# Storing m tiles 61 and 62 of a matmul-minus-matrix kernel in two transfers, of 120 and of 8 partitions

## The chip, the core and the metric

The kernel runs on one core of a Trainium2 chip. A core has a matrix engine (TensorE, PE in the profile) with its weight loads (PEld), a vector engine (VectorE, DVE), a scalar engine (ScalarE, ACT), GpSimd (POOL) and SyncE (SP), which here issues every DMA. The transfers are carried out by 16 DMA engines that the whole core shares. The metric is the device time of one execution in microseconds; the median over several runs is compared. The profile of one execution comes with its own time.

## The reference

```python
x:         (16, 512, 1024) float32     # 8192 rows of 1024 in all
weight:    (1024, 768)     float32
sub_value: (16, 512, 768)  float32
out = (np.matmul(x, weight) - sub_value).astype(np.float32)
```

## The kernel before

The 8192 rows are cut into 64 m tiles of 128 rows. Rows are not dealt to tiles in sequence: in each stretch of eight tiles (1024 rows) partition p holds eight consecutive rows, one for each tile. So one partition's rows of several neighbouring tiles lie next to each other in HBM, and a transfer of n tiles moves one run of n x 3,072 bytes for each partition (n x 4,096 bytes for x). This is what `view` (line 128) builds.

One m tile passes through these steps. Its x rows land in `x_ring` (16 slots). ScalarE casts them to fp16 (`cast`, L317). They are transposed, on TensorE for most tiles (`transposes`, L335, and a ScalarE copy out of PSUM, L348) and on VectorE for 18 of them (`transposes_dve`, L368). Then come 16 matmuls of 384 columns into `po_b` (`matmuls`, L198 and the weight loads of L397). The rows of sub_value have meanwhile landed in `so_ring` (32 slots); `finish` (L417) subtracts them on VectorE from the product, in place, and the slot then holds the output. From there it is stored.

All transfers are issued by SP in the order of the hand-written list `TRANSFERS` (line 29): loads of x, weight ("w") and sub_value ("s") and stores ("o") of mostly eight tiles each. The last entries are

```python
    ('o', 24, 8), ('o', 32, 8), ('s', 56, 8), ('o', 40, 8), ('o', 48, 8), ('o', 56, 5),
    ('o', 61, 2), ('o', 63, 1),
```

so the last three stores take tiles 56 to 60, tiles 61 and 62, and tile 63. `issue` (line 241) writes SP's instruction for each entry: a wait, for a store on the `finish` of its last tile, and one DMA instruction (L298; L262 for the weights). Each transfer signals a semaphore, called a lane, that `lane` (line 229) hands out; every lane counts to 16 for one transfer.

At the end (lines 520 to 527) SP first waits for every lane that nothing has waited for yet, but for the lane of the last store. Then the section is closed, with a barrier over all engines, and only after it SP waits for the last store, that of tile 63:

```python
    for one in left:
        if one is not last:
            nc.sync.wait_ge(one["sem"], one["value"])
    section.close()
    with tc.tile_critical(sync_engine=mybir.EngineType.SP, no_gpsimd_drain=True):
        nc.sync.wait_ge(last["sem"], last["value"])
```

Of the kernel before, what the change touches and what calls it, by code (L numbers as in the profile page):

```python
# [8 lines left out]
P = 128  # L9
# [5 lines left out]
NX, NSO = 16, 32  # L15
# [21 lines left out]
]  # L37


class Queue:  # L40
# [65 lines left out]
def kernel(  # L106
# [7 lines left out]
    nc = tc.nc  # L114
# [3 lines left out]
    out_flat = out.flatten_outer_dims()  # L118

    M_TOT, K = x_flat.shape  # L120
    _, N = weight.shape
    n_mt = M_TOT // P
# [5 lines left out]
    def view(flat, at, n):  # L128

        first, size = next(one for one in SEGMENTS if one[0] <= at < sum(one))  # L130
        assert at + n <= first + size
        rows = flat[first * P : (first + size) * P].rearrange("(p j) c -> p j c", p=P, j=size)
        return rows[:, at - first : at - first + n]
# [6 lines left out]
    def sbuf(name, shape, dtype):  # L140
        return ctx.enter_context(nc.sbuf_tensor(name, shape, dtype)).ap()
# [11 lines left out]
    so_ring = sbuf("so_ring", [P, NSO, N], F32)  # L153
# [11 lines left out]
    counter = {}  # L165
# [4 lines left out]
    def count(name):  # L170
        so_far[name] += 1
        return (counter[name], 1)

    sp, pe = Queue(nc, nc.sync), Queue(nc, nc.tensor)
    act, dve, pool = Queue(nc, nc.scalar), Queue(nc, nc.vector), Queue(nc, nc.gpsimd)
# [6 lines left out]
        out=along, data0=ones, data1=ones, initial=0.0, op0=mybir.AluOpType.mult, op1=mybir.AluOpType.add,  # L182
    ), waits=[(counter["ident"], 1)], then=count("ident"))
    dve.add(lambda: nc.vector.transpose(across, along), waits=[(counter["ident"], 3)], then=count("ident"))  # L184
    for a in range(P // Q):
        here = slice(a * Q, (a + 1) * Q)
        dve.add(lambda here=here: nc.vector.tensor_tensor(  # L187
            out=ident[here, here], in0=along[here], in1=across[here], op=mybir.AluOpType.is_equal,
# [16 lines left out]
    landed = {}  # L205
    cast_at, evac_at, pair_at, turn_at, mul_at, finish_at, w_at = {}, {}, {}, {}, {}, {}, {}
# [16 lines left out]
    done = {"w": set(), "x": set(), "s": set(), "o": set(), "cast": set(), "finish": set()}  # L223
    staged = {}
    lanes = []
    of_x, of_s, of_o = {}, {}, {}
    known = set()

    def lane(tag):

        for one in lanes:
            if one["tags"] <= known:
                break
        else:
            one = {"sem": tc.alloc_semaphore(f"lane{len(lanes)}"), "value": 0, "tags": set()}
            lanes.append(one)
        one["value"] += 16
        one["tags"].add(tag)
        return one["sem"], one["value"]

    def issue():
        nonlocal known
        while todo:
            kind, at, n = todo[0]
            span = set(range(at, at + n))
            old = {t - NX if kind == "x" else t - NSO for t in span}
            need, by = {
                "w": (set(), "o"),
                "x": ({t for t in old if t >= 0}, "cast"),
                "s": ({t for t in old if t >= 0}, "o"),  # L250
                "o": (span, "finish"),
            }[kind]
            if not need <= done[by]:
                return
            todo.pop(0)
            done[kind] |= span
            if kind == "w":

                first = NSO - 2 * (n_c - at)
                st = so_ring[:, first : first + 2]  # L260
                sem, value = lane((kind, at))
                sp.add(lambda st=st, at=at: nc.sync.dma_start(out=st, in_=w_c[at]), then=(sem, 16))  # L262
                for r in range(2):
                    dve.add(
                        lambda at=at, r=r, st=st: nc.vector.tensor_copy(out=w_sb[:, at, r], in_=st[:, r]),  # L265
                        waits=[(sem, value)], then=count("w"),
                    )
                    staged[first + r] = so_far["w"]
                w_at[at] = so_far["w"]
                continue  # L270
            ring, size, flat = {
                "x": (x_ring, NX, x_flat), "s": (so_ring, NSO, sub_flat), "o": (so_ring, NSO, out_flat)
            }[kind]
            here = ring[:, at % size : at % size + n]
            there = view(flat, at, n)
            waits = []
            if kind == "x" and need:
                waits.append((counter["cast"], max(cast_at[t] for t in need)))
                last = max(need, key=lambda t: cast_at[t])
                known |= {tag for t, tag in of_x.items() if t in cast_at and cast_at[t] <= cast_at[last]}  # L280
            if kind == "s":
                for t in need:
                    waits.append(landed["o", t])
                    known.add(of_o[t])
                for t in span:
                    if t % NSO in staged:
                        waits.append((counter["w"], staged.pop(t % NSO)))
                        known |= {("w", c) for c in w_at if w_at[c] <= waits[-1][1]}
            if kind == "o":
                waits.append((counter["finish"], max(finish_at[t] for t in need)))  # L290
                known |= {of_s[t] for t in finish_at if finish_at[t] <= max(finish_at[u] for u in need)}
            sem, value = lane((kind, at))
            for t in span:
                landed[kind, t] = (sem, value)
                {"x": of_x, "s": of_s, "o": of_o}[kind][t] = (kind, at)
            if kind == "o":
                here, there = there, here
            sp.add(lambda here=here, there=there: nc.sync.dma_start(out=here, in_=there), waits, (sem, 16))  # L298

    def cast(mi):  # L300
        assert mi in done["x"]
        done["cast"].add(mi)
        x_in = x_ring[:, mi % NX]
        first = mi - mi % 2
        waits = [landed["x", mi]]
        if first in ON_DVE:
            if mi == first:
                b, before = take("x16p", N16P, mi)
                if before is not None:
                    waits.append((counter["pair"], pair_at[before]))  # L310
            to = x16p_b[:, slot["x16p", first], mi - first]
        else:
            b, before = take("x16", N16, mi)
            if before is not None:
                waits.append((counter["turn"], turn_at[before]))
            to = x16_b[:, b]
        act.add(lambda: nc.scalar.copy(out=to, in_=x_in), waits, count("cast"))  # L317
        cast_at[mi] = so_far["cast"]
        issue()
# [92 lines left out]
    def finish(mi):  # L412
        assert mi in done["s"]
        done["finish"].add(mi)
        o = so_ring[:, mi % NSO].rearrange("p (h n) -> p h n", h=2)
        po = po_b[:, slot["po", mi]]
        dve.add(lambda: nc.vector.tensor_tensor(  # L417
            out=o, in0=po[:, :, :NS], in1=o, op=mybir.AluOpType.subtract
        ), [landed["s", mi], (counter["mul"], mul_at[mi])], count("finish"))
        finish_at[mi] = so_far["finish"]  # L420
        issue()

    issue()


# [59 lines left out]
    for mi in range(HEAD + (EARLY is not None), n_mt):  # L485
# [3 lines left out]
        t = mi + TA  # L489
# [32 lines left out]
    for one in left:  # L522
        if one is not last:
            nc.sync.wait_ge(one["sem"], one["value"])
    section.close()
    with tc.tile_critical(sync_engine=mybir.EngineType.SP, no_gpsimd_drain=True):
        nc.sync.wait_ge(last["sem"], last["value"])
# [30 lines left out]
```

## Time and profile before

| | |
|---|---|
| median of 4 runs | 210.36 us (210.15 to 210.57) |
| profiled execution, its time | 210.45 us |
| profiled execution, its span | 208.6 us |
| PE busy | 195.4 us (94%) |
| DVE busy | 128.2 us (61%) |
| ACT busy | 109.0 us (52%) |
| the DMA queue's packets, share of 16 engines | 97.8% |
| bytes moved | 87.08 MB, 417 GB/s over the span |
| store of tiles 56 to 60: 1,920 KB, issue to landing | 10.1 us |
| store of tiles 61 and 62: 768 KB, issue to landing | 6.2 us |
| store of tile 63: 384 KB, issue to landing | 4.5 us |

The span runs from the first to the last instruction; the time of a run has some two microseconds more around it. A busy share is an average over the whole span, and engines overlap. "Issue to landing" runs from the start of SP's DMA instruction to the last of the sixteen completions of that transfer. The DMA share counts the time that packets took, over 16 engines; 1.00 is all sixteen busy, and one engine alone is 0.06.

### The profile page before, as it was taken

To read this page: it belongs to the slowest core of one execution; us is meant where nothing else is said; L and a number is where in the kernel's file an instruction comes from. 1 tells how busy PE (TensorE), PEld (TensorE's weight loads), DVE (VectorE), ACT (ScalarE), POOL (GpSimd) and SP (SyncE) were. 2 spreads that over 40 slices of the span, in tenths; PEclk is the share of its full clock that TensorE was granted. 3 is DMA by queue.
4 is the path that set the end of the run, shared out by engine and by line. 5 is a ranking of instruction groups with operands and counts; after the bars stand their busy time and mean duration, and the time that the engine had idled before them with its cause. 6 is when DMAs were issued, how large, how long until landed. Compare 5 with 4: busy or idle time off the path is not lost.

```text
span 208.6 us, 2612 instructions
## 1 busy us (share of the span) xinstructions
PE 195.4 (94%) x1234; PEld 75.5 (36%) x700; DVE 128.2 (61%) x224; ACT 109.0 (52%) x113; POOL 1.0 (0%) x7
## 2 busy tenths in 40 slices
PE   6999699969999999999999999999999999999960
PEld 0234243324434433443443443343344344334310
DVE  2323224975994795598399379469839938952330
ACT  3555659506673761944645576193564737507300
POOL 1000000000000000000000000000000000000000
PEclk9999999999999999999999999999999999999997
DMA  6999999999999999999999999999999999999993
GB/s 210 417 426 431 435 426 429 459 423 421 434 446 459 375 429 448 446 408 432 467 408 424 448 415 424 471 426 418 430 454 399 435 443 434 410 443 448 410 413 124
DMA packets 5476, 87.08 MB, mean 417 GB/s; under 512 B 608, under 2 KB 608, under 8 KB 1888
## 3 DMA queue, kind: packets, MB, share of 16 engines
q1 hardware_dynamic: 5472, 87.03, 97.8%
q8 instruction: 1, 0.02, 0.0%
q14 instruction: 3, 0.02, 0.0%
HBM read 61.87 MB, written 25.17 MB: 417 GB/s over the span
## 4 chain that ended last, share of the span: by engine, by line
PE 75%; DMA 13%; DVE 6%; SPq 3%; issue 1%; DVEq 0%
PE po_b L198 67%; DMA so_ring<-in_sub_value_dram 13%; PE pt_b L335 8%; DVE xtp_b L368 3%; DVE so_ring L417 2%; SPq L298 2%; SPq L262 1%; SPq L553 0%; DVEq L59 0%; SPq L138 0%
## 5 line engine op out<-in xcount | busy, mean ns | idle before, releaser
L198 PE MATMUL po_b<-w_sb,xt_b 128*128 128x384 f16 x704 | 126.0, 326 | 0.9 <-DVE w_sb L265 0.8
L417 DVE TENSOR_TENSOR so_ring<-po_b,so_ring 128x768 f32<-128x768 f32 x64 | 60.8, 957 | 59.5 <-PE po_b L198 40.0
L348 ACT COPY xt_b<-pt_b 128x1024 f16<-128x1024 f16 x44 | 44.5, 1012 | 65.7 <-PE pt_b L335 64.8
L368 DVE STREAM_TRANSPOSE xtp_b<-x16p_b 32x256 f32<-32x256 f32 x144 | 62.7, 435 | 2.3
L198 PE MATMUL po_b<-w_sb,xtp_b 128*128 128x384 f16 x320 | 61.3, 326 | 1.9 <-DVE xtp_b L368 1.7
L397 PEld LDWEIGHTS <-xt_b 128*128 128x128 f16 x352 | 34.4, 98 | 58.6 <-issue 55.3
L317 ACT CAST x_b<-x_ring 128x1024 f16<-128x1024 f32 x46 | 47.2, 1048 | 4.8 <-DMA x_ring<-in_x_dram 4.8
L335 PE MATMUL pt_b<-ident,x_b 128*128 128x128 f32 x184 | 47.5, 274 | 1.9 <-ACT x_b L317 1.8
L335 PEld LDWEIGHTS pt_b<-ident,x_b 128*128 128x128 f32 x184 | 25.4, 141 | 45.0 <-issue 36.6
L317 ACT CAST x16p_b<-x_ring 128x1024 f16<-128x1024 f32 x18 | 18.8, 1046 | 14.8 <-DMA x_ring<-in_x_dram 14.8
L397 PEld LDWEIGHTS <-xtp_b 128*128 128x128 f16 x160 | 15.7, 98 | 20.4 <-issue 18.3
L265 DVE CAST w_sb<-so_ring 128x768 f16<-128x768 f32 x8 | 4.1, 557 | 11.6 <-DMA so_ring<-in_weight_dram 11.6
L198 PE MATMUL po_b<-idle_x,idle_w 128*128 128x512 f16 x26 | 7.9, 454 | 1.7 <-POOL idle_x L178 1.7
L348 ACT COPY xtp_b<-pt_b 128x1024 f16<-128x1024 f16 x2 | 2.0, 1012 | 2.5 <-PE pt_b L335 2.5
L317 ACT ACT_TABLE_LOAD x1 | 1.3, 1283 | 0.9 <-SPq L138 0.9
L427 PEld LDWEIGHTS <-idle_w 128*128 128x128 f16 x4 | 0.4, 100 | 1.7 <-POOL idle_x L178 1.7
L187 DVE TENSOR_TENSOR ident<-along,across 32x32 f32<-32x32 f32 x4 | 0.7, 183 | 0.1
L179 DVE MEMSET ones<- 128x32 f32 x1 | 0.1, 85 | 1.0 <-SPq L138 1.0
L178 POOL MEMSET idle_x<- 128x512 f16 x1 | 0.5, 530 | 0.0
L499 ACT CAST stub<-ident 128x1 f16<-128x1 f32 x2 | 0.4, 194 | 0.0
L184 DVE STREAM_TRANSPOSE across<-along 128x32 f32<-128x32 f32 x1 | 0.2, 211 | 0.0
L476 POOL MEMSET mark<- 128x1 f32 x1 | 0.1, 99 | 24.0 <-ACT xtp_b L348 24.0
(7 smaller groups left out, 1.0 us busy)
## 6 DMA issues: line engine op xcount, KB each, us to landing
so_ring<-in_sub_value_dram SPq DMA_DIRECT2D x7, 3072.0 KB, 24.2
out_dram<-so_ring SPq DMA_DIRECT2D x7, 3072.0 KB, 26.6
x_ring<-in_x_dram SPq DMA_DIRECT2D x5, 4096.0 KB, 23.1
x_ring<-in_x_dram SPq DMA_DIRECT2D x2, 2048.0 KB, 27.6
so_ring<-in_weight_dram SPq DMA_DIRECT2D x4, 768.0 KB, 8.4
x_ring<-in_x_dram SPq DMA_DIRECT2D x1, 3072.0 KB, 28.6
x_ring<-in_x_dram SPq DMA_DIRECT2D x2, 1024.0 KB, 25.0
out_dram<-so_ring SPq DMA_DIRECT2D x1, 1920.0 KB, 10.1
```

The costliest lines, as they stand in the source:

```text
L178: pool.add(lambda: nc.gpsimd.memset(idle_x, 0.0), then=count("idle"))
L187: dve.add(lambda here=here: nc.vector.tensor_tensor(out=ident[here, here], in0=along[here], in1=across[here], op=mybir.AluOpType.is_equal, ...
L198: return nc.tensor.add_instruction(mybir.InstMatmult(name=nc.get_next_instruction_name(), engine=full.engine, ins=list(full.ins), outs=lis ...
L262: sp.add(lambda st=st, at=at: nc.sync.dma_start(out=st, in_=w_c[at]), then=(sem, 16))
L265: lambda at=at, r=r, st=st: nc.vector.tensor_copy(out=w_sb[:, at, r], in_=st[:, r]),
L298: sp.add(lambda here=here, there=there: nc.sync.dma_start(out=here, in_=there), waits, (sem, 16))
L317: act.add(lambda: nc.scalar.copy(out=to, in_=x_in), waits, count("cast"))
L335: pe.add(lambda: nc.tensor.transpose(words, from_, ident), waits, count("turn") if last else None)
L348: act.add(lambda: nc.scalar.copy(out=to, in_=pt_b[:, b]), waits, count("evac"))
L368: dve.add(lambda: nc.vector.transpose(xt[b * Q : (b + 1) * Q, :, a * Q : (a + 1) * Q], x16[a * Q : (a + 1) * Q, :, b * Q : (b + 1) * Q],), ...
L397: pe.add(lambda weights=weights: nc.tensor.ldweights(weights, tile_position=(0, 0)), [w for w in waits if w[0] in ready])
L417: dve.add(lambda: nc.vector.tensor_tensor(out=o, in0=po[:, :, :NS], in1=o, op=mybir.AluOpType.subtract), [landed["s", mi], (counter["mul"] ...
```

## The change

The store of tiles 61 and 62 becomes two transfers on the same queue, of partitions 0 to 119 and of partitions 120 to 127. Both move two tiles (6,144 bytes for a partition). Every other transfer stays as it was, and so does the order of the list. The first part carries the wait on `finish`; the second follows it at once. Each part gets a lane of its own, so one more lane is waited for at the end. The code for entries of kind "q" and the list `own` belong to the edit too, but no entry of `TRANSFERS` has this kind, so they emit nothing.

```diff
+SPLIT = {61: ((0, 120), (120, 128))}
...
             if kind == "o":
                 waits.append((counter["finish"], max(finish_at[t] for t in need)))
                 known |= {of_s[t] for t in finish_at if finish_at[t] <= max(finish_at[u] for u in need)}
-            sem, value = lane((kind, at))
+            if kind == "o":
+                here, there = there, here
+            for low, high in SPLIT.get(at, ((0, P),)) if kind == "o" else ((0, P),):
+                sem, value = lane((kind, at))
+                sp.add(lambda here=here[low:high], there=there[low:high]: nc.sync.dma_start(
+                    out=here, in_=there
+                ), waits, (sem, 16))
             for t in span:
                 landed[kind, t] = (sem, value)
                 {"x": of_x, "s": of_s, "o": of_o}[kind][t] = (kind, at)
-            if kind == "o":
-                here, there = there, here
-            sp.add(lambda here=here, there=there: nc.sync.dma_start(out=here, in_=there), waits, (sem, 16))
...
+    for sem in own:
+        nc.sync.wait_ge(sem, 16)
     section.close()
```

On SP the one instruction for 128 partitions of 1,536 elements is replaced by two, for 120 and for 8 partitions of 1,536 elements. No other engine's instructions change.

More of the change, by code (lines that the diff above doesn't have):

```diff
@@ L227 @@
     known = set()
+    own = []
     def lane(tag):
@@ L251, in issue @@
                 "o": (span, "finish"),
+                "q": (span, "finish"),
             }[kind]
@@ L255, in issue @@
             todo.pop(0)
-            done[kind] |= span
+            done["o" if kind == "q" else kind] |= span
+            if kind == "q":
+                here, there = so_ring[:, at % NSO : at % NSO + n], view(out_flat, at, n)
+                waits = [(counter["finish"], max(finish_at[t] for t in need)), landed["s", n_mt - 1]]
+                for low, high in OWN:
+                    own.append(tc.alloc_semaphore(f"own{low}"))
+                    pool.add(lambda low=low, high=high, here=here, there=there: nc.gpsimd.dma_start(
+                        out=there[low:high], in_=here[low:high], max_dma_last_dim=4 * N,
+                    ), waits, (own[-1], 16))
+                continue
             if kind == "w":
```

## The prediction

> **What bounds the kernel now.** I read the page's slices first, for the resource that is full over the whole span.
>
> ```profile
> span 208.6 us, 2612 instructions
> PE   6999699969999999999999999999999999999960
> DMA  6999999999999999999999999999999999999993
> GB/s 210 417 426 431 435 426 429 459 423 421 434 446 459 375 429 448 446 408 432 467 408 424 448 415 424 471 426 418 430 454 399 435 443 434 410 443 448 410 413 124
> DMA packets 5476, 87.08 MB, mean 417 GB/s; under 512 B 608, under 2 KB 608, under 8 KB 1888
> ```
>
> PE and DMA are both full from the second slice on; in the last slice PE has nothing and DMA still 0.3. So the end is a tail of transfers. The 608 packets under 512 bytes are completions: section 6 of the page adds up to 38 transfers, and 608 / 38 = 16. Every transfer thus runs on all 16 DMA engines, and 128 partitions give each of them 8 rows and a completion. Next, the end of the chain of waits (start, length, what):
>
> ```profile
> 196.56 5.21 PE po_b L198 x32
> 201.77 0.02 issue
> 201.79 0.96 DVE so_ring L417
> ```
>
> The chain that the profile follows ends with the last subtraction at 201.79 + 0.96 = 202.75, yet the span ends at 208.62. From section 6 and the store issues, at 194.4, 200.2 and 202.8: the store of tiles 61 and 62 lands at 200.18 + 6.2 = 206.4, that of tile 63 at 202.78 + 4.5 = 207.3. Then the windows of the tail (the last two numbers are the DMA share of 16 engines and GB/s):
>
> ```profile
> 203.00:203.50 0.50, 0.00 (x0) 0.00 (x0) 0.00 (x0) 0.00 (x0) 0.00 (x0) 1.00 0.99 418
> 204.50:205.00 0.50, 0.00 (x0) 0.00 (x0) 0.00 (x0) 0.00 (x0) 0.00 (x0) 1.00 0.46 184
> 205.45:205.95 0.50, 0.00 (x0) 0.00 (x0) 0.00 (x0) 0.00 (x0) 0.00 (x0) 1.00 0.18 74
> 205.95:206.45 0.50, 0.00 (x0) 0.00 (x0) 0.00 (x0) 0.00 (x0) 0.00 (x0) 0.92 0.12 49
> 206.45:207.00 0.55, 0.00 (x0) 0.00 (x0) 0.00 (x0) 0.00 (x0) 0.00 (x0) 0.50 0.06 22
> 207.00:208.62 1.62, 0.00 (x0) 0.00 (x0) 0.00 (x0) 0.00 (x0) 0.00 (x0) 0.50 0.00 0
> ```
>
> This is the view that matters. At 203 all sixteen work; from 205.45 three (0.18 x 16 = 2.9), from 205.95 two (1.9), and from 206.45 to 207.00 one engine alone (1.0). The trace's completion records of tile 63's store say the same: eleven of sixteen by 205.27, then 205.64, 205.76, 206.43, 206.78, 207.32. The kernel ends on one late DMA engine, 0.54 behind the next. Last, SP's waits:
>
> ```profile
> SPq L524 <- DMA out_dram<-so_ring: 3.1, 1, 3.1
> SPq L553 <- DMA out_dram<-so_ring: 0.2, 1, 0.2
> ```
>
> L524 waits until 206.4, for tiles 61 and 62; the wait for tile 63 is only 0.2 long, ending at its landing (207.3). In between SP closes the section, about 0.75. So there are two ways to the end: the last landing of tile 63, and the last landing of tiles 61 and 62 plus 0.75, which is 0.2 shorter.
>
> **The change part by part.** The price of a row: 418 GB/s at a share of 0.99 is 418 / (16 x 0.99) = 26.4 GB/s an engine, so a row of 6,144 bytes takes 0.233 us, eight take 1.86, and eight rows of tile 63 (3,072 bytes) 0.93.
>
> *Removed and added on SP.* One DMA instruction becomes two. An issue takes 0.33 (the store issues of the tail, 332 to 333 ns). The second starts at about 200.55 and is done by 200.9, and the next instruction waits for the last subtraction until 202.78. So 1.9 us of waiting hide it; without that cover it would cost 0.33 to 0.4. No other queue is passed: PE, DVE and ACT end at 202.75, and none waits for a store any more. One more lane is waited for before the section closes. Those waits stand some 0.06 apart in the trace; this hides in the 0.2 of slack, and would cost 0.06 without it.
>
> *Moved: who carries which row.* No transfer of other than 128 partitions is in this trace, so how 120 rows are dealt is bounded from both sides. If an engine keeps its eight rows, 120 rows fill 15 engines, and one is left out: its queue is shorter by 1.86. If the rows are spread over all sixteen again, an engine carries 7 or 8, and the last one saves 0 to 0.23. The other eight rows may go one each to eight engines (+0.24 there with the completion), or all to one (+1.86). I take 15 engines and one row each on eight: 8 rows an engine is what all 38 transfers show.
>
> [...]
>
> *Is the late engine the one left out?* This decides the sum. In the packet records of the very first transfer the sixteen engines begin between 1.95 and 2.66 us, and the chain of packets that completes last there (4.48) begins 15th, at 2.59. In the first eight transfers the last completion already stands 0.08 to 0.15 after the last but one, and one engine stays last from then on, so far as the sixteen completions of each transfer can be followed. If engines are served in turn, the late one is of the last served, and 120 rows leave out the last. I give this 0.6, against 1/16 by mere count.
>
> *The sum.* The late engine would be done at 207.00 - 1.86 = 205.14, far from the end. Then the next engine ends the span: 207.32 - 206.78 = 0.54 earlier if it carries none of the eight rows, 0.54 - 0.24 = 0.30 earlier if it does. Eight of fifteen carry one; but if they are the first served and late engines the last served, the next one is likelier to be spared. I take 0.54 with two parts, 0.30 with one: 0.46, rounded up to 0.5. The other way to the end: tiles 61 and 62 land with the next engine, at 206.39 - 0.54 = 205.85, plus 0.75 and 0.06 is 206.66, still under 206.78. Profiled execution: 210.45 - 0.5 = 209.95; it stands 0.09 above the median of the runs, so 210.36 - 0.5 = 209.85.
>
> *What the pace of a row may do.* Another dealing changes which engine reads which partitions. A gain is excluded, as the engines work at 0.99 already. For a loss the farthest row is the first 5 us of the span, 203 GB/s at a share of 0.60: 203 / (16 x 0.60) = 21.1 GB/s, 0.291 a row, 1.25 times. On eight rows that is +0.47. I keep the pace of the tail, the row nearest in kind (stores of the same size), and 1.25 for the range.
>
> [...]
>
> **The rivals.**
> 1. *The wrong engine is freed, at the same pace.* For it: nothing in the profile numbers the engines. Against: the late one begins among the last. The late engine keeps its rows, with no extra row (0) or one (+0.24): 210.36 to 210.60.
> 2. *Slower: the rows of the 120 are read at a slower pace.* Place: those eight rows on the engine that ends last. For it: the dealing over engines is new and the queue's share has no room left. Against: the pace is even all through, 375 to 471 GB/s by slices. At 1.25 times, with the right engine freed and one extra row, -0.30 + 0.47 = +0.17 (210.53); with the wrong one freed, +0.24 + 0.47 = +0.71 (211.07). It makes the kernel slower by 0.42 from 1.10 times on if the late engine still has its rows and an extra one ((0.42 - 0.24) / 1.86), and from 1.5 times if it is freed ((0.42 + 0.54) / 1.86).
> 3. *The change doesn't do what it says:* the 120 rows are spread over sixteen engines again. The late engine saves 0 to 0.23 and may get a row of the eight: 210.1 to 210.6, no change.
>
> **How the numbers follow.** Forecast 0.48, rival 1 0.18, rival 2 0.27, rival 3 0.07. A difference under 0.2% (0.42 us) can't be told from none in this kernel. Faster by more than that: three quarters of the forecast and a little of the others, 0.38. Slower: most of rival 2, 0.23. Within: 0.39, from the forecast with the extra row, rivals 1 and 3, and the rest of 2. The time is the forecast's, 209.85; its own range is 209.7 to 210.15 (0.54 and 0.30, with 0.1 of scatter). The range for 8 in 10 reaches over rival 1 and to most of rival 2: 209.7 to 210.9.
>
> **What would show it.** Right: completions under 512 bytes rise from 608 to 608 + 15 + 8 - 16 = 615; the stretch of one engine alone (share 0.06) is gone from the tail or shorter; tile 63's store lands 4.0 us after its issue and the wait of L524's place shrinks by half a microsecond. A total of 624 would be rival 3. Rival 1 shows as 615 with the lone engine still at 207.0 or later. Rival 2 shows as packets of the split store above 0.25 us, and three or more engines busy at 206.5. I am wrong altogether if PE's or VectorE's end (202.75) moves, for nothing before 200.2 changes.

## The result, and the profile after

The changed kernel takes 210.91 us (median of 42 runs, 210.11 to 212.07), the kernel before 210.49 us in the same comparison (64 runs, 210.09 to 210.96). The ratio is 1.0026 with a 95% interval of 1.0019 to 1.0033: slower by 0.55 us, where 0.5 us faster had been forecast. The spread has grown too, from 0.9 to 2.0 us.

The page of the changed kernel (span, the DMA's busy tenths in 40 slices, and its packets), from an execution of 210.26 us:

```profile
span 208.4 us, 2614 instructions
DMA  5999999999999999999999999999999999999994
DMA packets 5483, 87.08 MB, mean 418 GB/s; under 512 B 615, under 2 KB 615, under 8 KB 1895
```

The packets under 512 bytes are now 615, that is 37 transfers with 16 completions, one with 15 and one with 8. So the two parts run on as many engines as was foreseen; which engine has which rows the records don't tell. The span is even 0.2 shorter than before: this execution is one of the fastest of the 42, and no loss is seen in it at first sight. The loss shows in how the packets run. The kernel before, in windows of the tail (length, busy time of the engines, clock, then DMA share of 16 engines and GB/s):

```profile
202.00:204.00 2.00, 0.00 (x0) 0.00 (x0) 0.75 (x1) 0.00 (x0) 0.00 (x0) 1.00 0.93 389
204.00:206.00 2.00, 0.00 (x0) 0.00 (x0) 0.00 (x0) 0.00 (x0) 0.00 (x0) 1.00 0.49 198
```

The changed kernel, in the same view:

```profile
202.00:204.00 2.00, 0.00 (x0) 0.00 (x0) 0.78 (x1) 0.00 (x0) 0.00 (x0) 1.00 0.91 343
204.00:206.00 2.00, 0.00 (x0) 0.00 (x0) 0.00 (x0) 0.00 (x0) 0.00 (x0) 1.00 0.68 257
206.45:206.82 0.37, 0.00 (x0) 0.00 (x0) 0.00 (x0) 0.00 (x0) 0.00 (x0) 0.50 0.09 33
```

Read the last two numbers together. GB/s divided by 16 x share is what a busy engine moves: 26.1 and 25.3 before, 23.6 and 23.6 after. The engines are busy, and move less. The packet records of the trace say it by the row (what one partition contributes to a transfer, one packet): before, the 128 rows of tiles 61 and 62 take 0.234 us on average and none more than 0.240; after, the mean is 0.263, seven of them take over 0.43 and the longest 0.92. The last window shows that the late engine, the one that ended the kernel before, is no longer alone: 0.09 x 16 is one and a half engines.

SP's waits of the changed kernel:

```profile
SPq L309 <- DVE so_ring L433: 20.0, 3, 12.8
SPq L540 <- DMA out_dram<-so_ring: 2.9, 1, 2.9
```

The wait for the split store (L540, L524 before) ends with its last completion at 206.21; what follows is the closing of the section as before. In another execution of the same kernel (210.0 us of span) the same line of the waits reads as follows:

```profile
SPq L540 <- DMA out_dram<-so_ring: 4.7, 1, 4.7
```

The windows of that execution show one engine alone up to 208.35 (0.06):

```profile
206.00:206.70 0.70, 0.00 (x0) 0.00 (x0) 0.00 (x0) 0.00 (x0) 0.00 (x0) 0.89 0.19 75
206.70:208.35 1.65, 0.00 (x0) 0.00 (x0) 0.00 (x0) 0.00 (x0) 0.00 (x0) 0.50 0.06 26
```

### The profile page after: what moved, and what is told of

The parts are those of the page before. It is cut to its first block, busy times and chain, and to the rows that moved or that the text cites. A ratio compares the mean times of both kernels' runs of the same rounds, so it can differ in the third digit from the quotient of the medians.

```text
span 208.4 us, 2614 instructions
## 1 busy us (share of the span) xinstructions
PE 195.2 (94%) x1234; PEld 75.5 (36%) x700; DVE 128.2 (62%) x224; ACT 109.0 (52%) x113; POOL 1.0 (0%) x7
## 4 chain that ended last, share of the span: by engine, by line
PE 75%; DMA 13%; DVE 6%; SPq 3%; issue 1%; DVEq 0%
PE po_b L200 67%; DMA so_ring<-in_sub_value_dram 13%; PE pt_b L351 8%; DVE xtp_b L384 3%; DVE so_ring L433 2%; SPq L309 2%; SPq L275 1%; SPq L571 0%; DVEq L61 0%; SPq L140 0%
## 5 line engine op out<-in xcount | busy, mean ns | idle before, releaser
L413 PEld LDWEIGHTS <-xtp_b 128*128 128x128 f16 x160 | 15.7, 98 | 20.4 <-issue 18.3
```

The costliest lines, as they stand in the source:

```text
L413: pe.add(lambda weights=weights: nc.tensor.ldweights(weights, tile_position=(0, 0)), [w for w in waits if w[0] in ready])
```

## The experiments

Three theories were set against each other. *Pace*: the rows of the parts of 120 and 8 partitions take longer, because, as the author supposed, the engines that have them share a way out of the on-chip memory. *Extra row*: the late engine keeps its rows, and it or its neighbour has one more. *Price of a transfer*: the added issue, lane and completions cost. The first four kernels ran on one chip, against 35 runs of the kernel before.

**e1: the changed kernel again.** No edit.

> The changed kernel again, as the reference for the others on this chip: about +0.55 us (ratio 1.002 to 1.004) if the chip is an average one. Pace theory (the rows of the 120 partitions are dealt to engines that then share a way out of the on-chip memory, and are read at a slower pace): the engines that start the split store together at 201.8 need clearly more than 1.87 us for their eight rows. Extra-row theory (the late engine keeps its rows, and it or its neighbour gets one row more): 1.87 us as before, and only an added 0.24.

1.0006 (0.9997 to 1.0016), under the 1.002 to 1.004 expected: no clear loss on this chip, though single runs went up to 211.8. The profile is the 210.0 us one shown above. Rows take 0.262 on average. The time alone decides nothing here.

**e2: the two tiles as two stores.**

```diff
-    ('o', 61, 2), ('o', 63, 1),
+    ('o', 61, 1), ('o', 62, 1), ('o', 63, 1),
-SPLIT = {61: ((0, 120), (120, 128))}
+SPLIT = {}
```

> Tiles 61 and 62 as two stores of 128 partitions: one more issue, lane and set of completions, but rows dealt as in every other transfer. Pace theory: no change against before (within 0.1 us). Extra-row theory: no change. Price-of-a-transfer theory (the added issue, lane and completions are what costs): slower like the change, +0.4 to +0.6.

0.9997 (0.9988 to 1.0006). All rows of the three last stores take 0.121 (they are 3,072 bytes), none above 0.125. One more transfer costs nothing here, so the price theory falls. The windows give 25.3 and 25.0 GB/s an engine:

```profile
202.00:204.00 2.00, 0.00 (x0) 0.00 (x0) 0.40 (x1) 0.00 (x0) 0.00 (x0) 1.00 1.01 409
204.00:206.00 2.00, 0.00 (x0) 0.00 (x0) 0.00 (x0) 0.00 (x0) 0.00 (x0) 1.00 0.55 220
```

**e3: 112 and 16 partitions.** By the author's estimate every engine keeps eight rows, 112 / 16 = 7 and 16 / 16 = 1, from other partitions.

```diff
-SPLIT = {61: ((0, 120), (120, 128))}
+SPLIT = {61: ((0, 112), (112, 128))}
```

> 112 and 16 partitions, which can both be dealt to all sixteen engines, 7 rows and 1: no engine freed, none with more than 8 rows, but the partitions that an engine reads are other ones. Pace theory: slower by 0.2 to 0.8, and the split store's rows above 0.25 us each. Extra-row theory: no change (within 0.1). Price-of-a-transfer theory: +0.4 to +0.6.

1.0017 (1.0008 to 1.0026), rows at 0.244 on average and up to 0.62. Slower, and by that estimate with no engine relieved or loaded: the extra-row theory doesn't give that, the pace theory does, with a time inside its 0.2 to 0.8 us and rows just under the 0.25 that it expected. The profile is of the fastest of these runs (210.51), and in it the late engine has lost nothing: from its last row of tiles 48 to 55 (200.04) to that of tiles 61 and 62 (206.45) it takes 6.41, as before the change.

**e4: the part of 120 alone.**

```diff
-SPLIT = {61: ((0, 120), (120, 128))}
+SPLIT = {61: ((0, 120),)}
```

> Only partitions 0 to 119 of tiles 61 and 62 are stored; the rows of partitions 120 to 127 of these two tiles are left out of the output. Pace theory: still slower than before, by 0.1 to 0.5. Extra-row theory: not slower, 0 to -0.5. Price-of-a-transfer theory: no change.

1.0011 (0.9998 to 1.0025), inconclusive in time. In its profile the last engine comes to its eight rows at 204.88 and is done at 207.56: 2.68 us, against 1.84 before. Rows take 0.266. So in this execution (211.62 us) the loss is there without the eight-row part. The windows of this profile, 24.3 and 22.2 GB/s an engine:

```profile
202.00:204.00 2.00, 0.00 (x0) 0.00 (x0) 0.54 (x1) 0.00 (x0) 0.00 (x0) 1.00 0.93 361
204.00:206.00 2.00, 0.00 (x0) 0.00 (x0) 0.00 (x0) 0.00 (x0) 0.00 (x0) 0.56 0.63 224
```

**e5: which engine is the late one.**

```diff
-SPLIT = {61: ((0, 120), (120, 128))}
+SPLIT = {61: ((0, 14), (14, 27), (27, 39), (39, 50), (50, 60), (60, 69), (69, 80), (80, 128))}
```

> The store of tiles 61 and 62 cut into parts of 14, 13, 12, 11, 10, 9, 11 and 48 partitions, to find which engine is the late one. If a part of n partitions runs on the n lowest engines, its completions are n, and the late engine is missing from every part that is smaller than its number plus one; it is seen in a part as a completion one to two microseconds after the others. If the late engine were the sixteenth (my prediction), no part but that of 48 has such a completion. If it is one of the ninth to fifteenth, the largest parts have it and the smaller ones don't. The time itself tells nothing here: eight issues of 0.33 to 0.45 us follow each other and reach past 202.8.

There is one execution of this kernel. The parts complete n times each, plus one record right after the issue where n is below 16. The last completions:

| part | tiles 56 to 60 | 14 | 13 | 12 | 11 | 10 | 9 |
|---|---|---|---|---|---|---|---|
| last completion, us | 204.46 | 204.69 | 204.93 | 205.17 | 205.41 | 205.02 | 205.26 |

From 204.46 to 205.41 the last completion advances by one row (0.24) for each part: the late engine has a row of each. The part of 10 is done before the part of 11: the late engine isn't in it. If a part of n partitions always takes the same first n engines, which these times fit and no record shows, it is the eleventh. Then 120 partitions, which leave out only the sixteenth, don't free it, and 8 don't load it. The profiles of the changed kernel fit: there the part of 8 is done (205.92 to 206.18) before the late engine ends the part of 120 (206.21 to 207.74).

**e6: 64 and 64 partitions.**

```diff
-SPLIT = {61: ((0, 120), (120, 128))}
+SPLIT = {61: ((0, 64), (64, 128))}
```

> 64 and 64 partitions, each dealt to sixteen engines, 4 rows each. No engine is freed and none has more than 8 rows. [...] Extra-row theory: rows at 0.234, no change of time.

Rows at 0.293 on average, up to 0.97, against 0.263 with the change and 0.234 before; time 1.0012 (0.9998 to 1.0027). The rows are slower, as in the pace theory and not in the extra-row theory; the time is unclear. The windows give 23.9 and 20.4 GB/s an engine:

```profile
202.00:204.00 2.00, 0.00 (x0) 0.00 (x0) 0.84 (x1) 0.00 (x0) 0.00 (x0) 1.00 0.94 359
204.00:206.00 2.00, 0.00 (x0) 0.00 (x0) 0.00 (x0) 0.00 (x0) 0.00 (x0) 0.91 0.78 254
```

**e7 and e8: the cuts in an eight-tile store**, where all sixteen engines are at work around it (shares of 0.91 to 1.09 in the windows from 190 to 200 us of the kernel before).

```diff
-SPLIT = {61: ((0, 120), (120, 128))}
+SPLIT = {48: ((0, 120), (120, 128))}      # e7
+SPLIT = {48: ((0, 112), (112, 128))}      # e8
```

> The same cut, 120 and 8 partitions, made in the eight-tile store of tiles 48 to 55 and not in that of 61 and 62: four times the bytes and all sixteen engines at work before and after it. Pace theory: the cut store's rows (24,576 bytes, 0.912 us before) take 1.1 to 1.8 us and the kernel is slower by 1 to 6 us. Extra-row theory: rows at 0.912, and +0.9 us at most (one more row on eight engines).

> 112 and 16 partitions in the store of tiles 48 to 55: every engine has its 8 rows, dealt differently. Pace theory: slower by 0.5 to 5 us. Extra-row theory: no change (within 0.1 us).

e7: 1.0356 (1.0329 to 1.0382), +7.7 us in the median. e8: 1.0225 (1.0184 to 1.0267), +5.3. Both lie above what the pace theory had at most (6 and 5), and are out of reach of the extra row (0.9 and 0). The rows of 24,576 bytes, 0.914 before, average 1.40 and 1.14 in the stretch after 188 us, and go up to 4.6 and 3.6. Two microseconds early in the big store, first in the windows of the kernel before:

```profile
192.00:194.00 2.00, 2.00 (x15) 0.91 (x8) 0.55 (x1) 0.92 (x2) 0.00 (x0) 1.00 0.97 418
```

The same window of e7:

```profile
192.00:194.00 2.00, 2.00 (x15) 0.78 (x8) 0.37 (x1) 0.92 (x2) 0.00 (x0) 1.00 1.02 258
```

All sixteen engines are busy in both, at 26.9 GB/s each before and 15.8 in e7. This is what slowed rows look like in such a view: share full, bytes missing.

**e9 to e12: on which side the pace is lost.** If engines share a way, as the pace theory supposes, it is on the side that is read or on the side that is written. The store of tiles 48 to 55 in sixteen transfers of 8 partitions, either neighbours or four apart, chosen for each side by itself. e9 is four apart on both sides, e10 neighbours on both, e11 reads neighbours and writes four apart, e12 the other way round.

```diff
-SPLIT = {61: ((0, 120), (120, 128))}
+STEP = [slice(g * 32 + a, g * 32 + 32, 4) for g in range(4) for a in range(4)]
+NEXT = [slice(8 * j, 8 * j + 8) for j in range(16)]
+SPLIT = {48: list(zip(STEP, STEP))}       # e10 (NEXT, NEXT), e11 (NEXT, STEP), e12 (STEP, NEXT)
...
-            for low, high in SPLIT.get(at, ((0, P),)) if kind == "o" else ((0, P),):
+            whole = [(slice(0, P), slice(0, P))]
+            for inner, outer in SPLIT.get(at, whole) if kind == "o" else whole:
                 sem, value = lane((kind, at))
-                sp.add(lambda here=here[low:high], there=there[low:high]: nc.sync.dma_start(
+                a, b = (outer, inner) if kind == "o" else (inner, outer)
+                sp.add(lambda here=here[a], there=there[b]: nc.sync.dma_start(
```

> [...] In this run the rows go where they belong. [...] Odd-shape theory (any transfer that isn't of 128 partitions is slow): rows of 1.1 us and more, as in the run with 120 and 8 partitions.

> The same with 8 neighbouring partitions in each transfer (0 to 7, 8 to 15, ..). [...]

> Read from 8 neighbouring partitions, written to the places in HBM of 8 partitions four apart (the output rows of tiles 48 to 55 are thereby permuted). If the sharing is on the side of the on-chip memory: as slow as with neighbours on both sides. If it is on the side of HBM: as fast as with four apart on both sides.

> Read from 8 partitions four apart, written to the places in HBM of 8 neighbouring partitions (the output rows of tiles 48 to 55 are permuted). If the sharing is on the side of the on-chip memory: as fast as with four apart on both sides, rows at 0.91 us. If it is on the side of HBM: as slow as with neighbours on both sides.

Medians of two runs each: 222.1, 229.2, 229.9 and 222.7 us, the kernel before 210.9. In these four it is the side that is read, the on-chip memory, that sets the pace (7.1 us between e9 and e10, 7.2 between e12 and e11); where the rows go in HBM changes 0.6 us, which two runs don't tell from none. Four microseconds early in that store, in the windows of e9:

```profile
192.00:196.00 4.00, 4.00 (x28) 1.75 (x16) 0.96 (x1) 1.35 (x2) 0.00 (x0) 1.00 0.52 218
```

Of e10:

```profile
192.00:196.00 4.00, 4.00 (x28) 1.68 (x15) 0.96 (x1) 1.43 (x2) 0.00 (x0) 1.00 0.53 166
```

Of e11:

```profile
192.00:196.00 4.00, 4.00 (x29) 1.81 (x17) 0.96 (x1) 1.11 (x2) 0.00 (x0) 1.00 0.51 154
```

Of e12:

```profile
192.00:196.00 4.00, 4.00 (x29) 1.69 (x16) 0.96 (x1) 1.42 (x2) 0.00 (x0) 1.00 0.48 203
```

Eight engines' worth of work (0.48 to 0.53 of 16) is seen in all four; which eight no record says. At eight engines they move 26.2 and 26.4 GB/s each when the eight partitions of a transfer are four apart, 19.6 and 18.9 when these are neighbours. The odd-shape theory does not fit these windows: all these transfers are of 8 partitions, and those four apart complete 0.92 apart in e9 at first, while the rows of e10 take 1.38 on average. The engines of e10 drift apart: the eight completions of the first part lie within 2.1 us, those of the sixth within 4.9. e9 is 11.2 slower than before: its transfers complete 0.92 apart until 199.5 us, and then 1.9 apart, soon after the store has come to partitions 64 to 127. By then the store of tiles 56 to 60 runs beside it, and all sixteen engines together move 208 GB/s at a share of 0.97, 13.4 an engine:

```profile
200.00:204.00 4.00, 1.56 (x10) 0.33 (x4) 0.96 (x1) 0.00 (x0) 0.00 (x0) 1.00 0.97 208
```

What slows them is not shown. The rows of tiles 56 to 60 take 1.1 to 1.2 us, twice their 0.574, already from about 196.5 on, when the split store still reads partitions 32 to 63 at its 0.91 a row; what holds them up there stays open too. The comparison of the four runs rests on the windows from 192 to 196 us, before that.

**f1 to f4: does the pace account for the 0.55?** The changed kernel and the kernel before, twice each on one chip, for their profiles. No edit.

> The changed kernel, for another profile. Pace theory: the late engine is in the part of 120 partitions and not in that of 8, and its eight rows take 1.87 to 2.7 us, never less; together with the two other profiles of this kernel the mean is 0.2 to 0.6 above 1.87. Late-arrival theory: the rows take 1.87 us, and what differs is when the late engine comes to the split store.

> The kernel before, for another profile. Pace theory: the late engine's eight rows of tiles 61 and 62 take 1.84 to 1.88 us, as in the first profile, whenever it comes to them. Late-arrival theory: the same; but it comes to them earlier (204.2 to 204.6) than in the changed kernel.

> The changed kernel once more, as in the first of these four runs: the pace theory expects 1.87 to 2.7 us for the late engine's eight rows, the late-arrival theory 1.87.

> The kernel before once more, as in the second of these four runs: both theories expect 1.84 to 1.88 us for the late engine's eight rows; the late-arrival theory expects it to come to them before 204.6.

f1 1.0022 (1.0002 to 1.0042), f3 1.0038 (1.0022 to 1.0054), f2 and f4 1.0001 both (0.999 to 1.0011, and 0.9991 to 1.0012). The last completions of four stores, from the trace:

| profile | tiles 48 to 55 | 56 to 60 | 61 and 62, the late engine | 63 | first to third |
|---|---|---|---|---|---|
| before | 199.98 | 204.55 | 206.39 | 207.32 | 6.41 |
| before (f2) | 200.04 | 204.61 | 206.46 | 207.39 | 6.42 |
| before (f4) | 199.97 | 204.57 | 206.38 | 207.32 | 6.41 |
| changed | 199.79 | 204.35 | 206.21 | 207.14 | 6.42 |
| changed (e1) | 200.54 | 205.58 | 207.74 | 208.67 | 7.20 |
| changed (f1) | 200.23 | 204.86 | 207.53 | 208.47 | 7.30 |
| changed (f3) | 200.19 | 205.16 | 207.38 | 208.32 | 7.19 |

The last column is the late engine's time for its rows of tiles 56 to 62. Before it is 6.41 or 6.42 in every profile; after it is 6.42, 7.20, 7.30 and 7.19, 0.61 more on average. These four executions are 0.80 longer than the three before on average (211.28 against 210.47 us), so the rows account for three quarters of it. The other 0.19 stands already in the first column, before the first row of the split store (201.8 to 202.0), and no run explains it. The measured 0.55 is a median over more runs, so the 0.61 gives its size and not its exact sum. Part of the 0.61 lies in the split store (1.86, 2.16, 2.67 and 2.22 us against 1.81 to 1.85), as the pace theory says. The late-arrival theory is half right: in three of the four the late engine also comes later to the split store, by up to 1.0 (205.58 against 204.55 to 204.61). Up to 0.47 of that arises in its rows of tiles 56 to 60, which are already slowed. Those rows of 15,360 bytes take 0.574 on average and 0.596 at most before; in e1 two of them took 0.776 and 0.865, in f1 one took 0.640 and in f3 one 0.992, from 203.6 on, while the other engines were at the split store. The windows of f1, 24.0 and 21.8 GB/s an engine, and one engine left after 207:

```profile
202.00:204.00 2.00, 0.00 (x0) 0.00 (x0) 0.59 (x1) 0.00 (x0) 0.00 (x0) 1.00 0.97 373
204.00:206.00 2.00, 0.00 (x0) 0.00 (x0) 0.00 (x0) 0.00 (x0) 0.00 (x0) 0.60 0.77 269
207.00:208.30 1.30, 0.00 (x0) 0.00 (x0) 0.00 (x0) 0.00 (x0) 0.00 (x0) 0.50 0.05 21
```

A version that frees the late engine and keeps the pace of the rows was not tried: every cut into two parts that was run also changed that pace (0.244 to 0.293 a row against 0.234 in the store of tiles 61 and 62, 1.40 and 1.14 against 0.914 in that of 48 to 55).

## Why the prediction was wrong

- *What bounds the kernel.* Right: the tail ends on one DMA engine, before and after, and PE and VectorE end where they did (VectorE at 202.78, 202.75 before).
- *SP's second issue is hidden.* Right. The two issues took 0.41 and 0.33 and were done at 201.0, the next one waited until 202.81. e2 shows that one more transfer costs nothing.
- *One more lane costs 0.06 in slack.* Right: SP passes one more wait, from 206.22 to 206.28, and still reaches the last wait before tile 63 lands.
- *15 engines, and one row each on eight.* Right: 615 completions, 0.24 for the extra row (an engine that is done with the part of 120 at 205.94 has its row of the other part at 206.18). It doesn't set the end: the late engine has no such row. In that profile it came near, though: the engine with the extra row ended 0.02 before the late one (207.12 and 207.14).
- *"Is the late engine the one left out?"* This step failed. I gave it 0.6 from the order in which engines begin and complete in the first transfers. The late engine is in the part of 120 in all four profiles of the changed kernel, and e5 puts it eleventh if the parts take the same first engines. Nor can the end be read from the start: in the kernel before the last completion stands 0.07 to 0.15 after the last but one in the first eight transfers, 0.47 in the one that lands at 29.69 and 0.91 in the next, at 34.26. Between these two one packet of 16,384 bytes of the queue for instructions (q8) takes 0.94 us, at 30.57. All seven profiles of the two kernels have this packet (29.8 to 31.3) and such a step (0.01 to 0.47 in the last transfer to land before it, 0.53 to 1.14 in the next); that the packet makes the late engine late is likely by this and not shown. With that the gain of 0.3 to 0.54 was gone: rival 1, at its lower end, 0.
- *"I keep the pace of the tail".* This step failed too, and it made the sign. The pace was taken from stores of 128 partitions, "the row nearest in kind", and the parts of 120 and 8 move at another pace. Rows take 1.12 to 1.17 times as long on average in the four profiles; for the late engine the loss is 0 to 0.9 us, 0.61 on average. Rival 2 named the slower rows and priced them at +0.47; its +0.71 for "the wrong one freed" has an extra row in it that the late engine did not get. That +0.47 is near the measured 0.55 is luck: its 1.25 came from the first 5 us, where only loads run, and it missed a place, the late engine's rows of the store before. The bound of 1.25 held for the mean of this small store, not for the late engine's eight rows in f1 (2.67 against 1.85) and not for the big store (1.40 / 0.914 = 1.53 times).
- *Why the rows are slower.* The runs show it in part: in the eight-tile store the engines moved 26.2 GB/s each with partitions four apart (e9) and 19.6 with neighbours (e10). How the rows of the part of 120 are dealt no record shows, so that they lose their pace in the same way is the author's inference. The engines come to the small store up to 2.5 us apart (tiles 56 to 60 land from 202.03 to 204.55 in the kernel before); that may be why its rows lose less (1.12 to 1.17 times) than those of the big one (1.53), and no run tests it.

## What to carry to other kernels

Cutting a transfer by partitions can slow the engines around it (e7 was 7.7 us slower), also in the transfer before (single rows of 0.640 to 0.992 against 0.574 in e1, f1 and f3); cut along the free axis instead (e2), where every transfer keeps 128 partitions and one more of them cost nothing (0.9997). Before moving rows away from a late engine, find out which one it is: parts of falling size, as in e5, can show it in one profile. And a row of the profile bounds a price only if it has the property in question; a full share of 128-partition transfers (26.9 GB/s an engine from 192 to 194 us) says nothing about another shape (15.8 in e7).

## What the runs showed of the hardware

- A DMA engine that is held up counts as busy: in e7 the share is 1.02 at 258 GB/s, before it is 0.97 at 418. Share and GB/s have to be read together.
- The slowing is on the side of the on-chip memory: in sixteen transfers of the eight-tile store, reading neighbours costs 7 us more than reading partitions four apart, whether the rows go to neighbouring places in HBM or not (229.2 and 229.9 against 222.1 and 222.7).
- The late engine ended the kernel before in each of three profiles within 0.1 us (207.32, 207.39, 207.32); after the change its end ranges over 1.5 us (207.14 to 208.67).
